# A third of the softmax pieces of eight blocks go to tiles of another pool, and expert numbers are read one by one

## The chip, the cores and the metric

The kernel runs on one core of a Trainium2 chip. Its engines each work through a list of their own, in order: TensorE (PE; PEld is its weight load), VectorE (DVE), ScalarE (ACT), GpSimd (POOL) and SyncE (SP), which only issues DMAs and reads numbers into registers. An instruction that has to wait holds up everything behind it on its engine. The metric is device time in microseconds. Before the change three runs took 2329.93, 2331.04 and 2335.01 us; the median is 2331.04 us.

## The reference, cut to what matters

One layer of an encoder for 2048 tokens of 1024 numbers: a mixer (differential attention with 4 heads, and gated linear attention), cross-attention to 256 memory tokens, and a mixture of 32 experts of which each token takes two. The two parts that the change touches are these:

```python
# differential attention, 16 query blocks of 128, chunk-causal
def probs(qb, kk):
    sc = jnp.einsum('bhqd,bhkd->bhqk', qb, kk).astype(jnp.float32) * scale
    return jax.nn.softmax(jnp.where(mask, sc, -jnp.inf), axis=-1)
p = probs(qb1, k1) - lam * probs(qb2, k2)
o = jnp.einsum('bhqk,bhkv->bhqv', p.astype(v.dtype), v)
...
# experts: tokens sorted by expert, each expert's rows through its own three matrices
hid = jax.nn.silu(xb @ w_gate[e]) * (xb @ w_up[e])
out = hid @ w_down[e]
```

## The kernel before, in words

**Recording and order.** The kernel doesn't issue its instructions as it is written. It records them with what each needs, and `flush` then puts them in one order for each engine: it plays the program through with a price for each instruction (`price`) and, at each step, takes what can start first, with a recorded number plus a table of shifts to break ties. Tiles belong to tags (pools); those of one tag are opened strictly in the order in which they were recorded, each when a buffer of the tag is free in that play. So a price or a tile's tag changes the order of instructions on every engine, though not what they compute.

**Attention (`stage_a2`).** Query blocks go from 15 down to 0; block i sees (i+1)*128 keys. For each of 4 heads there are two score maps (s = 0, 1). `scores` multiplies queries `qT` with keys `KC` into PSUM banks `sc` (4 buffers, up to 512 keys each), VectorE takes the extreme of each (`mx`, `m`), and ScalarE writes the exponentials into the pieces `e`, one tile for each 1024 keys: two for blocks 15 to 8, one for blocks 7 to 0. All pieces come from tag "E", 8 buffers of 4 KB per partition. `combine` forms the difference of the two maps: VectorE into the first map's piece, ScalarE casts to half precision in the second map's piece, GpSimd writes the remainder there, and a DMA transposes the result to `pT`. `values` multiplies `pT` with values `VC`. A buffer of tag "E" is free when the GpSimd subtraction (first map) or the DMA transpose (second map) has read it.

**Tag "W".** 28 buffers of 4 KB. In attention they hold keys (`KC`, 8), values (`VC`, 8), the query weights `wq` (4) and the output weights `wo` (8). As the blocks go down, the keys and values of the highest blocks are used no more and their buffers come free. Recorded next on this tag, in `begin_c` ahead of block 0, are the cross-attention's keys `kv` (2) and query weights `wcq` (8), 512 KB each from memory.

**Cross-attention and routing (`stage_c`)** go block by block; each block's routing appends its tokens to the experts' lists in memory (`lists<-row,dest`, an indirect DMA from GpSimd, each after the one before has landed).

**Experts (`stage_moe`).** Experts 0 and 1 and a list of leftovers are fixed. Then `rank` sorts the other 30 by their number of tokens, and writes their numbers into the tile `order`. For each, `chosen` has SP read one number of `order` into a register (`value_load`; in the rows TENSOR_LOAD, then a register operation and a check, ISA), `fetch` loads 128 list entries at a time (`lt<-lists`) and gathers the tokens (`ex<-xnS,lt`, tag "Q", 4 buffers), and `split_expert` loads the expert's weights in 12 pieces of 512 KB (`est`, tag "E", 8 buffers), which ScalarE and VectorE split into two half-precision parts (`ew`, tag "W"). The register tells where `lt` and `est` read. All `est` and `lt` are issued from SP. `fetch` is called two experts ahead of use.

Of the kernel before, what the change touches and what calls it, by code (L numbers as in the profile page):

```python
# [19 lines left out]
S = 2048  # L20
# [16 lines left out]
PT0 = 1  # L37
AHEAD = 4
GATE0 = 6
FTAG = "W"  # L40
# [64 lines left out]
class Program:  # L105
# [121 lines left out]
    def price(self, o, outs, ins):  # L227
# [3 lines left out]
        if m == "value_load":  # L231
            return 100
        if o.dma:
# [164 lines left out]
class Layer:  # L398
# [541 lines left out]
    def stage_a2(self):  # L940
# [4 lines left out]
        self.wo = [self.stored("wo", self.woS[4 * n:4 * n + 4]) for n in range(2)]  # L945
        blocks = self.blocks
        heads = [(j, h) for j in range(NB) for h in range(4)]
        for x, y in zip(heads + [None], [None] + heads):
# [72 lines left out]
    def scores(self, B, h, s):  # L1021
# [19 lines left out]
        self.prog.group = "se" if n > 1024 else "SE"  # L1041
        e = B["e", h, s] = [self.tile("E", "e", [w], F32) for _, w in B["chunks"]]
        for c, (b, k0, w) in enumerate(sc):
# [435 lines left out]
    def stage_moe(self):  # L1479
# [3 lines left out]
        slots += [k + j * n for k in range(n) for j in range(3)]  # L1483
        ready, rows = {}, {}

        def fetch(n):

            s = slots[n]
            if n == 0:
                which, need = lambda: NE, ()  # L1490
            elif n < FIXED:
                which, need, _ = self.second
            else:
                if n == FIXED:
                    self.rank()
                which, need = self.chosen(s)
            self.prog.shift = FRONT
            rows[n] = which, need, self.fetch(CAPS[s], which, need)
            self.prog.shift = 0

# [17 lines left out]

    def chosen(self, rank):

        reg = []
        need = [self.prog.call("sync", lambda nc: reg.append(nc.sync.value_load(
            self.order[0:1, rank:rank + 1], min_val=0, max_val=NE - 1)), [], [self.order], method="value_load")]
        return (lambda: reg[0]), need
# [31 lines left out]
    def fetch(self, cap, which, need, first=None, blocks=0):  # L1556
# [4 lines left out]
        for t0 in range(0, cap, 128):  # L1561
# [7 lines left out]
            def load(nc, lt=lt, m=m, t0=t0, parts=parts):  # L1569
# [7 lines left out]
                if parts > 1:  # L1577
# [3 lines left out]
            x = self.tile("Q", "ex", [2, D], F16)  # L1581
            prog.call("gpsimd", lambda nc, x=x, lt=lt, g=g: nc.gpsimd.indirect_dma_start(  # L1582
                out=x[:g].rearrange("p t d -> p (t d)"), out_offset=None, in_=self.xnS[:S + OFF - blocks * 128],
                in_offset=bass.IndirectOffsetOnAxis(ap=lt[:g, 0:1], axis=0)), [x[:g]],
                      [lt[:g], self.xnS[:S + OFF - blocks * 128]])
            rows.append((t0, n, x, m, lt, parts))
# [133 lines left out]
```

## Time and profile before

| | us |
|---|---|
| median of three runs | 2331.04 |
| profiled execution | 2337.98 |
| its span | 2336.2 |
| PE busy | 2133.3 (91%) |
| DVE busy | 1543.2 (66%) |
| ACT busy | 1341.4 (57%) |
| POOL busy | 775.1 (33%) |

The span is the profiled execution from its first instruction to its last, and 1.78 us of the execution lie around it. Busy shares are means over stages that have different limits: attention runs from about 620 to 1200 us, cross-attention from there to about 1600, the experts from there to the end. Block 11's scores begin at about 810 us, block 7's at 965, block 3's at 1070.

### The profile page before, as it was taken

To read this page: it belongs to the slowest core of one execution; us is meant where nothing else is said; L and a number is where in the kernel's file an instruction comes from. 1 tells how busy PE (TensorE), PEld (TensorE's weight loads), DVE (VectorE), ACT (ScalarE), POOL (GpSimd) and SP (SyncE) were. 2 spreads that over 40 slices of the span, in tenths; PEclk is the share of its full clock that TensorE was granted. 3 is DMA by queue.
4 is the path that set the end of the run, shared out by engine and by line. 5 is a ranking of instruction groups with operands and counts; after the bars stand their busy time and mean duration, and the time that the engine had idled before them with its cause. 6 is when DMAs were issued, how large, how long until landed. Compare 5 with 4: busy or idle time off the path is not lost.

```text
span 2336.2 us, 56192 instructions
## 1 busy us (share of the span) xinstructions
PE 2133.3 (91%) x22161; PEld 1463.9 (63%) x22161; DVE 1543.2 (66%) x3439; ACT 1341.4 (57%) x2850; POOL 775.1 (33%) x814
## 2 busy tenths in 40 slices
PE   6999998999988888889998999997699999999898
PEld 3456655565544544545575777865587877777776
DVE  7354355654578878887645665458477878877884
ACT  6455355554466666666433333345477777777774
POOL 1445235552155555455312222213221222222201
PEclk9999999999989999999999999998899999999999
DMA  9544346674457777677984675574799999999995
GB/s 259 158 119 105 95 114 190 187 204 119 119 110 152 154 162 163 155 174 181 207 209 121 141 168 115 125 215 141 248 327 352 361 353 366 359 349 359 361 357 143
DMA packets 500089, 484.52 MB, mean 207 GB/s; under 512 B 387202, under 2 KB 397596, under 8 KB 499820
## 3 DMA queue, kind: packets, MB, share of 16 engines
q1 hardware_dynamic: 485788, 441.06, 64.7%
q0 software_dynamic: 14032, 39.82, 7.1%
q8 instruction: 175, 2.87, 0.5%
q14 instruction: 94, 0.77, 0.1%
HBM read 306.35 MB, written 83.74 MB: 167 GB/s over the span
## 4 chain that ended last, share of the span: by engine, by line
PE 40%; DVE 8%; DMA 7%; issue 3%; ACT 3%; POOL 2%; SPq 1%; POOLq 0%; ACTq 0%; DVEq 0%
PE pgu L171 13%; PE py L171 8%; PE phc L171 6%; PE pc L171 6%; PE ph L171 2%; DMA est<-in_w_e_down_dram 2%; DVE mx L171 2%; ACT ew L171 2%; PE pxT L171 2%; PE pcs L171 2%; DMA pT<-e 1%; DVE e L171 1%; DMA xTr<-xc 1%; DVE ew L171 1%; PE sc L171 1%
## 5 line engine op out<-in xcount | busy, mean ns | idle before, releaser
L171 DVE SCALAR_TENSOR_TENSOR ew<-est,ew 128x1024 f16<-128x1024 f32 x384 | 461.5, 1220 | 97.8 <-ACT ew L171 88.0
L171 PE MATMUL pgu<-exT,ew 128*128 128x160 f16 (+27 forms) x6336 | 446.4, 225 | 3.0 <-issue 2.2
L171 PEld LDWEIGHTS <-ew 128*128 128x128 f16 x6336 | 403.9, 98 | 11.3 <-issue 4.8
L171 ACT ACTIVATE ew<-est 128x1024 f16<-128x1024 f32 x384 | 395.2, 1051 | 13.8 <-DMA est<-in_w_e_down_dram 7.8
L171 PEld LDWEIGHTS <-uT 128*128 128x128 f16 x1920 | 187.2, 98 | 226.0 <-issue 9.8
L171 POOL TENSOR_TENSOR e<-e 128x256 f16<-128x256 f32 (+1 forms) x288 | 201.0, 727 | 190.9 <-ACT e L171 107.7
L171 PE MATMUL py<-ew,hid 128*128 128x512 f16 (+4 forms) x1560 | 245.4, 349 | 19.7 <-DVE hid L171 14.3
L171 DVE TENSOR_REDUCE mx<-sc 128x1 f32<-128x512 f32 (+3 forms) x320 | 185.5, 603 | 67.9 <-PE sc L171 67.4
L171 ACT ACTIVATE e<-sc,m 128x512 f32<-128x512 f32 (+3 forms) x288 | 179.0, 630 | 73.2 <-DVE m L171 34.6
L171 PE MATMUL sc<-KC,qT 128*128 128x512 f16 (+3 forms) x640 | 174.9, 367 | 42.7 <-ACT e L171 40.3
L171 PE MATMUL ph<-wo,mT 128*128 128x512 f16 x768 | 193.9, 383 | 9.6 <-DMA mT<-gS 4.7
L171 PE MATMUL pc<-hT,wcq 128*128 128x128 f16 x3072 | 191.2, 219 | 1.4 <-DMA hT<-hcS 0.8
L171 PEld LDWEIGHTS <-wcq 128*128 128x128 f16 x3072 | 179.8, 98 | 4.7 <-DMA hT<-hcS 1.3
L171 PEld LDWEIGHTS <-hid 128*128 128x128 f16 (+4 forms) x1560 | 105.7, 104 | 120.7 <-issue 17.9
L171 PE MATMUL phc<-wco,prT 128*128 128x512 f16 x768 | 176.5, 383 | 4.3 <-DMA prT<-prc 4.3
L171 PE MATMUL po<-VC,pT 128*128 128x128 f16 x1632 | 130.2, 226 | 9.6 <-DMA pT<-e 5.0
L171 PEld LDWEIGHTS <-pT 128*128 128x128 f16 x1632 | 109.7, 102 | 37.5 <-DMA pT<-e 14.6
L171 PEld LDWEIGHTS <-prT 128*128 128x128 f16 x768 | 74.3, 99 | 86.5 <-DMA prT<-prc 4.4
L1660 POOL DMA_INDIRECT out_dram<-ey,lt x33 | 55.5, 1681 | 219.6 <-ACT ey L171 191.4
L1582 POOL DMA_INDIRECT ex<-xnS,lt x52 | 63.9, 1228 | 194.2 <-PE pxT L171 139.1
L171 PEld LDWEIGHTS <-mT 128*128 128x128 f16 x768 | 72.7, 98 | 86.2 <-DMA mT<-gS 7.0
L171 PEld LDWEIGHTS <-qT 128*128 128x128 f16 x640 | 60.4, 101 | 97.2 <-issue 57.7
(324 smaller groups left out, 3671.6 us busy)
## 6 DMA issues: line engine op xcount, KB each, us to landing
est<-in_w_e_gate_dram SPq DMA_DIRECT2D x128, 512.0 KB
est<-in_w_e_up_dram SPq DMA_DIRECT2D x128, 512.0 KB
est<-in_w_e_down_dram SPq DMA_DIRECT2D x128, 512.0 KB
wst<-in_w_in_dram SPq DMA_DIRECT2D x20, 512.0 KB
xt<-in_x_dram SPq DMA_DIRECT2D x16, 512.0 KB
uS<-uT SPq DMA_DIRECT2D x16, 512.0 KB
ust<-in_w_ckv_dram SPq DMA_DIRECT2D x16, 512.0 KB
uT<-uS SPq DMA_DIRECT2D x16, 512.0 KB
```

What stands on the lines that cost most here:

```text
L171: o.fn = fn or (lambda nc: getattr(getattr(nc, eng), method)(*a, **k))
L1582: prog.call("gpsimd", lambda nc, x=x, lt=lt, g=g: nc.gpsimd.indirect_dma_start(out=x[:g].rearrange("p t d -> p (t d)"), out_offset=None, i ...
L1660: self.prog.call("gpsimd", lambda nc: nc.gpsimd.indirect_dma_start(out=out, out_offset=bass.IndirectOffsetOnAxis(ap=rows, axis=0), in_=y, ...
```

## The change

Two edits. First, for blocks 11 to 4 every third piece `e` (counted over all blocks) is a tile of tag "W" in place of "E". Second, the read of a ranked expert's number is priced at 570 in place of 100 in the ordering, and from the third ranked expert on it needs, in the ordering, the token gather of the expert two places ahead of it; so the 30 reads don't stand side by side any more. No instruction is added or taken away.

```diff
+FEWER = range(4, 12)
...
         if m == "value_load":
-            return 100
+            return 570
...
+        self.made = 0
...
-        e = B["e", h, s] = [self.tile("E", "e", [w], F32) for _, w in B["chunks"]]
+        e = B["e", h, s] = []
+        for _, w in B["chunks"]:
+            self.made += 1
+            tag = "W" if self.made % 3 == 0 and B["i"] in FEWER else "E"
+            e.append(self.tile(tag, "e", [w], F32))
...
-        ready, rows = {}, {}
+        ready, rows, gathers = {}, {}, []
...
-                which, need = self.chosen(s)
+                which, need = self.chosen(s, gathers[n - 2:n - 1] if n > FIXED + 1 else [])
...
             rows[n] = which, need, self.fetch(CAPS[s], which, need)
+            gathers.append(self.gathered)
...
-    def chosen(self, rank):
+    def chosen(self, rank, after):
...
-            self.order[0:1, rank:rank + 1], min_val=0, max_val=NE - 1)), [], [self.order], method="value_load")]
+            self.order[0:1, rank:rank + 1], min_val=0, max_val=NE - 1)), [], [self.order], after, method="value_load")]
```

Line numbers of the changed kernel are higher by 1 to 9. Where the instructions went is seen at three places.

SP before, where the ranked experts begin: after the last weights of expert 1 that could be issued, 30 reads of `order` stand in a row (L1522), then ten loads of lists (L1579), and only then weights again (L1547).

```order
L1547 DMA est_3276<-in_w_e_down_dram 128x1024
L1522 TENSOR_LOAD order_3352
L1522 ISA x2
...
L1579 DMA lt_3337<-lists_1034 128x1x2
L1579 DMA lt_3339<-lists_1034 128x2
...
L1579 DMA lt_3481<-lists_1034 128x1x2
L1547 DMA est_3278<-in_w_e_down_dram 128x1024
L1547 ISA
L1547 DMA est_3387<-in_w_e_gate_dram 128x1024
```

The same place on SP now: two reads (L1531), seven loads of lists (L1588), then the same weights.

```order
L1556 DMA est_3276<-in_w_e_down_dram 128x1024
L1531 TENSOR_LOAD order_3352
L1531 ISA x2
...
L1588 DMA lt_3337<-lists_1034 128x1x2
L1588 DMA lt_3339<-lists_1034 128x2
...
L1588 DMA lt_3385<-lists_1034 128x1x2
L1556 DMA est_3278<-in_w_e_down_dram 128x1024
L1556 ISA
L1556 DMA est_3387<-in_w_e_gate_dram 128x1024
```

28 reads and three loads of lists have left the place between `est_3276` and `est_3278`.

SP now, further on, between an expert's weights: each of the 28 reads stands with its expert's one or two loads of lists, among the 12 weight pieces of another expert.

```order
L1556 DMA est_3438<-in_w_e_gate_dram 128x1024
L1531 TENSOR_LOAD order_3352
L1531 ISA x2
L1588 ISA
L1588 DMA lt_3432<-lists_1034 128x2
...
L1588 DMA lt_3481<-lists_1034 128x1x2
L1556 ISA
L1556 DMA est_3440<-in_w_e_gate_dram 128x1024
```

Before, these loads of lists stood among the weights too, without a read.

SP before, in attention while block 5 and block 4 are worked on: the last two of the ten cross-attention loads, `wcq`, stand alone between transposes; the eight others stand in the same way in earlier blocks.

```order
L171 DMA hcS7_1134<-hc_2087 128x2048
L171 DMA wcq_2503<-wcqS6_154 128x2048
L171 DMA_TRANSPOSE pT_2211<-e_2202 128x12x128
L171 DMA_TRANSPOSE mT_2165<-mcd_2164 128x8x128
L171 DMA wcq_2504<-wcqS7_155 128x2048
L171 DMA_TRANSPOSE pT_2234<-e_2216 128x12x128
L171 DMA_TRANSPOSE mT_2246<-gS5_102 128x8x128
L171 DMA_TRANSPOSE qT_2224<-qc_2223 128x16x128
```

The same place now (`qT_2224` is the transposed query of block 3):

```order
L172 DMA_TRANSPOSE mT_2246<-gS5_102 128x8x128
L172 DMA kv0_2495<-kvS0_268 128x2048
L172 DMA kv1_2496<-kvS1_269 128x2048
L172 DMA wcq_2497<-wcqS0_148 128x2048
...
L172 DMA wcq_2502<-wcqS5_153 128x2048
L172 DMA_TRANSPOSE qT_2224<-qc_2223 128x16x128
L172 DMA uT_2298<-uS2_83 128x2048
L172 DMA wcq_2503<-wcqS6_154 128x2048
```

All ten loads of tag "W" now come after the last piece `e` of that tag; eight of them stand side by side ahead of the query of block 3, and the two others soon after. In attention from block 11 to block 1 the order on PE, DVE, ACT and POOL differs too; in cross-attention, to the first gathers of the experts, it is the same on every engine.

## Rows read from the trace of the kernel before

**Rows 1.** Busy time by stage: stretch, us, each engine (x instructions), clock, DMA share, GB/s.
```profile
core 0: us, PE busy (x) PEld busy (x) DVE busy (x) ACT busy (x) POOL busy (x), PEclk, DMA share, GB/s
795.00:965.00 170.00, 144.26 (x1056) 82.29 (x1056) 135.89 (x293) 108.54 (x280) 86.50 (x115) 0.94 0.73 158
965.00:1085.00 120.00, 103.77 (x756) 57.75 (x754) 100.13 (x249) 78.78 (x205) 61.73 (x80) 0.97 0.75 168
1085.00:1200.00 115.00, 112.90 (x1092) 75.00 (x1090) 73.09 (x210) 55.70 (x149) 40.36 (x54) 1.00 0.85 185
1200.00:1560.00 360.00, 352.17 (x4096) 260.25 (x4094) 195.70 (x703) 135.57 (x350) 80.77 (x123) 0.99 0.62 152
1625.00:1655.00 30.00, 11.97 (x74) 5.33 (x75) 11.58 (x41) 4.57 (x9) 8.47 (x6) 0.69 0.13 30
1690.00:2280.00 590.00, 556.21 (x7312) 452.46 (x7311) 464.28 (x631) 447.52 (x669) 130.31 (x87) 0.97 1.02 355
```

**Rows 2.** SP in order of time, 1616 to 1658: start, us, instruction.
```profile
1616.96 5.29 SPq L1547 DMA_DIRECT2D est<-in_w_e_down_dram  x3
1646.13 6.50 SPq L1579 DMA_DIRECT2D lt<-lists  x10
1652.74 0.40 SPq L1547 DMA_DIRECT2D est<-in_w_e_down_dram  x1
1653.41 3.88 SPq L1547 DMA_DIRECT2D est<-in_w_e_gate_dram  x4
```

**Rows 3.** The reads of line 1522: count, duration ns, first and last start us.
```profile
L1522 SPq TENSOR_LOAD <-order x30: 261/266/476, 1628.3 to 1645.4; - x30
```

**Rows 4.** Other engines in order of time, 1609 to 1651, idle before in brackets.
```profile
1609.67 0.96 POOL L1403 DMA_INDIRECT lists<-row,dest  x1 [1.41 <-DMA lists<-row,dest]
1621.83 7.18 POOL L1403 DMA_INDIRECT lists<-row,dest  x1 [1.60 <-DMA lists<-row,dest]
1628.10 0.17 DVE L171 CAST order<-prk 1x32 int32<-1x32 f32 x1
1648.59 0.21 DVE L171 TENSOR_SCALAR dst<-lt,part 128x1 int32<-128x1 int32 x1 [14.88 <-DMA lt<-lists]
1650.67 6.05 PE L171 MATMUL py<-ew,hid 128*128 128x512 f16 x50 [14.34 <-DVE hid L171]
```

**Rows 5.** What SP waited for, 1690 to 2280: us in total, times, longest.
```profile
SPq L1547 <- DVE ew L171: 161.5, 155, 3.7
```

**Rows 6.** The chain of waits: start, us, what.
```profile
1743.83 7.54 DMA lt<-lists
```

**Rows 7.** Waits of ACT and PE, 795 to 965: us in total, times, longest.
```profile
ACT e L171 <- POOL e L171: 10.3, 8, 1.9
ACT e L171 <- DMA pT<-e: 8.1, 3, 4.8
PE sc L171 <- ACT e L171: 20.6, 16, 3.7
```

**Rows 8.** ACT and PE in order of time, two of those waits each.
```profile
825.21 0.69 ACT L171 ACTIVATE e<-sc,m 128x512 f32<-128x512 f32 x1 [1.76 <-POOL e L171]
826.04 0.59 PE L171 MATMUL sc<-KC,qT 128*128 128x512 f16 x2 [1.70 <-ACT e L171]
...
962.06 0.69 ACT L171 ACTIVATE e<-sc,m 128x512 f32<-128x512 f32 x1 [4.78 <-DMA pT<-e]
962.89 0.59 PE L171 MATMUL sc<-KC,qT 128*128 128x512 f16 x2 [1.21 <-ACT e L171]
```

**Rows 9.** Cross-attention's loads, then block 3's query and the first scores that use it.
```profile
L171 SPq DMA_DIRECT2D kv<-kvS x2: 324/324/325, 748.0 to 791.4; - x2
...
L171 SPq DMA_DIRECT2D wcq<-wcqS x8: 324/450/531, 813.8 to 1072.2; - x8
...
1084.98 1.88 SPq L171 DMA_TRANSPOSE qT<-qc  x1
...
1089.35 0.38 PE L171 MATMUL sc<-KC,qT 128*128 128x512 f16 x1
```

More of the change, by code (lines that the diff above doesn't have):

```diff
@@ L1581, in fetch @@
             x = self.tile("Q", "ex", [2, D], F16)
-            prog.call("gpsimd", lambda nc, x=x, lt=lt, g=g: nc.gpsimd.indirect_dma_start(
+            self.gathered = prog.call("gpsimd", lambda nc, x=x, lt=lt, g=g: nc.gpsimd.indirect_dma_start(
                 out=x[:g].rearrange("p t d -> p (t d)"), out_offset=None, in_=self.xnS[:S + OFF - blocks * 128],
                 in_offset=bass.IndirectOffsetOnAxis(ap=lt[:g, 0:1], axis=0)), [x[:g]],
-                      [lt[:g], self.xnS[:S + OFF - blocks * 128]])
+                                      [lt[:g], self.xnS[:S + OFF - blocks * 128]])
             rows.append((t0, n, x, m, lt, parts))
```

## The prediction

> **What bounds the kernel now.** I read the busy times by stage first, then, where a stage has a hole, each engine in order of time, and last the waits. In the table by stage [rows 1] the reader is to see four different limits. From 795 to 1085 us, in attention, no engine is full: PE is busy 144.26 of 170 us and DVE 135.89 of 170, then 103.77 and 100.13 of 120, so waits between engines set the pace. From 1085 to 1560 PE is busy 112.90 of 115 and 352.17 of 360 us: PE is the limit. From 1625 to 1655 nothing is: PE is busy 11.97 of 30 us and the DMA engines 0.13 of the time. From 1690 to 2280 the DMA engines show a share of 1.02 at 355 GB/s: transfers set the pace there, with PE close behind (556.21 of 590).
>
> The hole at 1625 to 1655 has one cause in SP's list. SP ends its last weight issue at 1616.96 + 5.29 = 1622.25 and issues its next DMA at 1646.13 [rows 2]. In between stand the 30 reads, from 1628.3 to 1645.4 [rows 3]: 17.1 us for 29 steps, 0.59 us each, of which the load itself is 0.266 and the rest is what goes with it. They could start when VectorE had written `order`, at 1628.10 [rows 4]. While they run, VectorE waits 14.88 us for a list that SP has not asked for, and TensorE 14.34 us for VectorE [rows 4]. So the last thing to end is SP's row of reads, and everything else is behind it.
>
> **Part one: the reads.** Now two reads stand there, and they end at 1628.3 + 2 x 0.59 = 1629.5. What is late next is the lists: the last scatter into them is on GpSimd from 1621.83 for 7.18 us, to 1629.01, and such a scatter landed 1.41 to 1.60 us after its issue ended [rows 4], so at about 1630.5. The first list load moves from 1646.13 to some 1630.6, 15.5 us earlier. Ten list loads took 6.50 us [rows 2], 0.65 each; seven now take 4.6, so the first weights go at 1635.2 where they went at 1652.74, 17.5 us earlier. Their buffers are free by then: VectorE's splits of what had been loaded were through but for one, which stood behind the wait of 14.88 us itself. I take the middle of the two shifts, 16.5 us, with 15.5 and 17.5 as ends.
>
> Does this reach the end? The list of work behind it is the same, and from 1655 on the DMA engines are full to 2280 [rows 1], so a stream of equal length that starts 16.5 us sooner ends 16.5 us sooner. If it is TensorE that paces some of that stage, it starts as much earlier, since its wait of 14.34 us ends with the same list.
>
> What comes back: the other 28 reads, 28 x 0.59 = 16.5 us on SP, now among the weight issues. The trace has no read of `order` inside that stage, so I bound it: nothing, if SP waits anyway, and 16.5 us, if each read delays the stream by its length. SP waits there for buffers that VectorE frees, 161.5 us in 155 waits [rows 5], so it is ahead of the stream; eight buffers of 512 KB in turn are 8 x 524288 bytes / 355 GB/s = 8 x 1.48 = 11.8 us of transfers, against a delay of 0.59 us once in an expert. That row is much nearer to nothing: I take 1 us. What is queued behind a read on SP are the list loads of the same expert and then weight pieces; who waits for them are the gather on GpSimd and the splits on ScalarE. The list is read an expert ahead of its gather, so I cost its later place at nothing here, and as a rival below. The one read of `total` (for the loop after the experts) moves up a little past weight pieces; it needs a sum that VectorE makes a few us after its wait ends, before SP gets there: nothing.
>
> Part one: 16.5 - 1 = 15.5 us, between -1 and 17.5.
>
> **Part two: the pieces of tag "W".** An exponential waits for a buffer when ScalarE waits for GpSimd's subtraction or for a transpose to read an older piece. Between 795 and 965 us these waits are 10.3 us in 8 and 8.1 us in 3 [rows 7], together 18.4. All lie in blocks 11 to 8, which take two pieces for each map; in blocks 7 to 4, one piece each, the same view shows none, so half of the edit has nothing to remove. What counts is whether PE then waits too. Of its 20.6 us behind ScalarE's exponentials [rows 7], six waits end 0.6 to 0.9 us after such a wait of ScalarE; the first and the last are the pairs in [rows 8], 1.70 and 1.21 us, and the six add up to 8.0. With a third of the pieces elsewhere, eight buffers serve twelve pieces, three heads in place of two, and I expect these waits to go. The gain is between nothing (VectorE, 80% busy, becomes what ScalarE waits for) and 18.4; I take 8, what PE itself waited.
>
> The same edit moves the ten loads of cross-attention's keys and weights. Before, they were issued one by one from 748.0 to 1072.2 [rows 9]; now eight stand ahead of block 3's query on SP. They are 8 x 1.48 = 11.8 us of transfers at the rate of the experts' stage, and in the trace that query had no slack: its transpose was issued at 1084.98 and the scores that use it ran at 1089.35 [rows 9]. The cost is between a gain (each earlier single load no longer stands before a transpose, up to 1.48 each, of which I count nothing) and 11.8 us, if the whole run is before the query and PE has nothing else. PE has output products and values to run in that place, and the loads can go while SP waits for the query; I take 4, a third, as nearer to the row that shows PE full there (112.90 of 115). Their own need is far off, in cross-attention.
>
> Part two: 8 - 4 = 4 us gained, between a loss of 12 and a gain of 18. It reaches the end because PE is the limit from 1085 to 1560 and its order there from block 0 on is unchanged.
>
> **Sum.** 15.5 + 4 = 19.5 us. The profiled execution took 2337.98 us (span 2336.2 and 1.78 around it), so 2318.5 in such an execution. The median of the three runs is 2331.04, 6.94 below the profiled one; I carry the same gain to it: 2311.5 us.
>
> **Rivals.**
> - *Attention loses.* The run of eight loads holds block 3's query, and the transposes behind it, for most of its 11.8 us, and the freed waits of ScalarE turn into waits for VectorE: a loss of 6 in place of a gain of 4. For it: no slack in [rows 9]. Against: PE's other work there. 2331.0 - 15.5 + 6 = 2321.5.
> - *Attention gains all of it.* All 18.4 us of buffer waits come off and the loads hide: 2331.0 - 15.5 - 18.4 = 2297. Against: VectorE at 80%, and five of the eleven waits had no wait of PE behind them.
> - *The reads are paid in full.* Each of the 28 holds the weight stream for its 0.59 us: 16.5 us come back, and attention's 4 are left, 2327. For it: the eight buffers may all be in use when SP reads. Against: [rows 5]. The Trainium skill (DMA: Bandwidth & Descriptors, section "Latency and other measured facts") gives a floor of about 600 ns for each such load, wherever it stands; the 0.59 us here agree, and by that rule alone an estimated 28 x 0.6 = 16.8 us stay on SP, and whether they are hidden no run here shows yet.
> - *The stall isn't the reads.* The lists land as late as before, and the reads only stood beside that wait. Then three list loads (2 us) and attention's 4 are won: 2325. Against: SP's first list load came 0.1 us after the last read's 0.59 us were over (1645.4 + 0.59 against 1646.13).
> - *Lists become the wait, and it is slower.* Read one by one, each list is loaded into full queues: one took 7.54 us to land and stood in the chain of waits [rows 6]. If its expert's gather waits for it, TensorE waits for the gather. From 19.5 / 28 = 0.7 us of open wait in each of 28 experts on, the change is slower; at 1 us it costs 28, and 2331.0 - 19.5 + 28 = 2339.5. Against: the order puts the read an expert ahead, some 20 us (590 us for 29 experts), against 7.54. The skill's same section has 2 us for a memory access at high load; the 7.54 us are far above it, and the measured one decides.
>
> **Chances.** Forecast 0.55, with a range of its own from 2303 to 2319 (attention from 12 gained to 4 lost). Attention loses 0.17, attention gains all 0.10, the reads paid in full 0.07, the stall isn't the reads 0.06, lists make it slower 0.05. The range 2300 to 2326 leaves out most of the case at 2297, the one at 2327 and the one at 2339.5, together under 0.2. A difference under 0.2%, 4.7 us, can't be told from none. Faster by more than that (under 2326.4): the forecast, both cases of attention, and about half of the two at 2325 and 2327, 0.88. Within it: the rest of those two, 0.07. Slower: 0.05.
>
> **What would show it.** Right on part one: SP's first ranked weights 17 us sooner after `order` is written than the 24.6 us of before (1628.10 to 1652.74), hence about 7; no wait of VectorE near 14.88 us; the stage at 355 GB/s as long as before. Wrong, if GB/s there falls with SP busy in reads, or GpSimd's gathers wait for lists far more than before. Right on part two: fewer waits of ScalarE for GpSimd and transposes between 795 and 965, and block 7's scores some 8 us sooner; then a wait of PE for block 3's query of about 4 us. The forecast is wrong as a whole if less than 10 us are gained between the write of `order` and the end, or attention loses more than 6.

## The result, and the profile after

| | before | after |
|---|---|---|
| median of four runs, us | 2330.83 | 2299.14 |
| lowest to highest, us | 2329.93 to 2335.01 | 2296.29 to 2301.12 |
| profiled execution, us (span) | 2337.98 (2336.2) | 2296.29 (2294.4) |

The ratio is 0.9866, with an interval of 95% from 0.9844 to 0.9888: 31.7 us faster, 1.3%. The prediction was 2311.5 us, a gain of 19.5; the direction is right, and the time lies under the predicted range.

The two profiled executions differ by 41.8 us of span. Cut at the first mask matmul of block 11, the last one of block 0, the write of `order`, the first ranked weight behind it and the last weight, that is:

| stretch | before, us | after, us | gained |
|---|---|---|---|
| start to block 11 | 817.69 | 819.85 | -2.2 |
| blocks 11 to 0 | 363.28 | 340.13 | 23.2 |
| end of block 0 to the write of `order` | 447.1 | 445.9 | 1.2 |
| write of `order` to first ranked weight | 24.64 | 6.77 | 17.9 |
| first ranked to last weight | 639.26 | 637.61 | 1.6 |
| last weight to the end | 44.2 | 44.1 | 0.1 |

So there are two gains, one of each edit. Before's profiled execution is 7 us above its median and after's is the lowest of its four, so about 10 of the 41.8 us are the scatter of executions.

**The reads.** The reads and the write of `order` in the changed kernel (count; shortest, median and longest duration in ns; first and last start in us), against [rows 3]:

```profile
L1531 SPq TENSOR_LOAD <-order x30: 270/460/1194, 1606.1 to 2175.2; - x30
L172 DVE CAST order<-prk x1: 172/172/172, 1605.9 to 1605.9; 1x32 int32<-1x32 f32 x1
```

The 30 reads no longer stand in a row of 17 us: they are spread over 570 us. SP in order of time there (start, us, instruction), against [rows 2]:

```profile
1594.77 5.29 SPq L1556 DMA_DIRECT2D est<-in_w_e_down_dram  x3
1608.01 4.58 SPq L1588 DMA_DIRECT2D lt<-lists  x7
1612.69 0.41 SPq L1556 DMA_DIRECT2D est<-in_w_e_down_dram  x1
1613.37 2.75 SPq L1556 DMA_DIRECT2D est<-in_w_e_gate_dram  x4
```

The first list goes 2.1 us after the write of `order` and the first weight 6.8 us after it. What is late now is the last scatter into the lists, as the prediction said; on GpSimd it is this row, against [rows 4]:

```profile
1598.75 8.07 POOL L1410 DMA_INDIRECT lists<-row,dest  x1 [0.72 <-DMA lists<-row,dest]
```

It ends at 1606.82, and SP's first list load follows at 1608.01, after a wait of 0.3 us for this scatter to land; so the two reads and the scatter now end almost together. VectorE's wait of 14.88 us for a list has become the wait of 1.9 us in this row (what VectorE waited for, 1600 to 1660 us: us in total, times, longest):

```profile
DVE dst L172 <- DMA lt<-lists: 1.9, 1, 1.9
```

And the stage behind it has the same rate as in [rows 1] (stretch, its length, busy time of each engine with its instructions, granted clock, share of the DMA engines, GB/s):

```profile
1603.00:1633.00 30.00, 20.74 (x354) 15.23 (x351) 18.77 (x57) 13.49 (x26) 11.14 (x8) 0.85 0.69 215
1648.00:2238.00 590.00, 562.71 (x7388) 457.61 (x7386) 468.74 (x640) 450.16 (x676) 133.29 (x88) 0.98 1.02 357
```

The 28 reads in it did not lower the 355 GB/s of before. SP still waits there for buffers, as in [rows 5] (us in total, times, longest, 1648 to 2238 us):

```profile
SPq L1556 <- DVE ew L172: 170.5, 166, 3.7
```

It is ahead of the stream, with reads or without.

**The pieces.** The same view by blocks: 11 to 8, 7 to 4, and the sum with blocks 3 to 0. First the kernel before:

```profile
817.69:979.62 161.93, 137.20 (x1014) 78.55 (x1013) 129.78 (x281) 103.03 (x261) 81.39 (x109) 0.94 0.72 160
979.62:1089.56 109.94, 96.80 (x710) 53.68 (x709) 89.67 (x225) 71.65 (x186) 58.04 (x76) 0.98 0.78 174
...
sum 363.28, PE 323.60 PEld 186.45 DVE 278.77 ACT 217.51 POOL 171.84; mean PE 107.87 PEld 62.15 DVE 92.92 ACT 72.50 POOL 57.28
```

Then the changed kernel:

```profile
819.85:951.59 131.74, 119.54 (x937) 68.24 (x936) 123.97 (x271) 100.46 (x258) 83.26 (x107) 1.00 0.85 173
951.59:1070.27 118.68, 108.04 (x810) 60.98 (x809) 95.09 (x245) 73.88 (x191) 58.46 (x79) 1.00 0.83 193
...
sum 340.13, PE 314.26 PEld 181.68 DVE 276.25 ACT 216.40 POOL 172.32; mean PE 104.75 PEld 60.56 DVE 92.08 ACT 72.13 POOL 57.44
```

Blocks 11 to 8 are 30.2 us shorter and blocks 7 to 4 are 8.7 longer. The counts of TensorE say that these 8.7 are no loss: 77 fewer matmuls stand in the first stretch and 100 more in the second. TensorE had filled its waits with other blocks' products, and these now come later. So it is the sum that counts, and it splits in two. TensorE's idle time went from 363.28 - 323.60 = 39.7 us to 340.13 - 314.26 = 25.9, which is 13.8 us. Its busy time for nearly the same work fell by 9.3 us; the granted clock of blocks 11 to 8 went from 0.94 to 1.00. As an estimate from the traces: over the three stretches TensorE was busy for 21.7 us at a clock of 0.50 before and for 3.4 us after, and half of the difference, 9.1 us, is what the slow clock cost, nearly all of the 9.3.

One pair of executions is little for that split. Of the runs below, the reads alone, the reads doubled and the second profile of before have, in attention, the order of instructions of the kernel before on all four engines; the pieces alone, the price alone, one read and three reads have that of the changed kernel. Blocks 11 to 0 take 358.8 to 363.3 us in the four profiles with the old order and 338.9 to 346.3 in the five with the new. By the means, 361.9 and 342.5, that is 19.4 us, of which 12.4 are TensorE's idle time and 7.0 its busy time (worked out as above, an estimated 6.2 of these are the clock's).

The waits of the changed kernel in blocks 11 to 8, against [rows 7]:

```profile
ACT e L172 <- DVE m L172: 19.9, 19, 2.6
ACT e L172 <- DVE e L172: 9.8, 13, 1.8
...
PE sc L172 <- ACT e L172: 7.1, 9, 2.2
```

ScalarE's waits for GpSimd and for transposes, 18.4 us of buffers, are gone altogether, and VectorE is what ScalarE waits for now. TensorE's waits behind exponentials, 20.5 us in blocks 11 to 8 before, are 7.1: not 8 of them went but 13.4. Of the 20.5 us only 8.1 stood right behind a buffer wait of ScalarE, the rest mostly behind its waits for VectorE; so at least 5.3 of the 13.4 us that went were not buffer waits themselves.

Where the clock's part comes from shows in stretches of 4 us. The kernel before, from 840 to 860:

```profile
840.00:844.00 4.00, 2.71 (x25) 1.59 (x24) 3.52 (x8) 2.85 (x8) 1.25 (x2) 1.00 0.78 148
844.00:848.00 4.00, 1.13 (x5) 0.33 (x5) 4.00 (x10) 2.00 (x4) 2.46 (x4) 0.95 0.74 180
848.00:852.00 4.00, 2.77 (x7) 0.89 (x7) 2.43 (x6) 2.33 (x8) 2.75 (x4) 0.50 0.63 118
852.00:856.00 4.00, 3.36 (x21) 2.26 (x21) 3.35 (x8) 2.93 (x8) 0.00 (x0) 0.50 0.08 17
856.00:860.00 4.00, 4.00 (x47) 3.21 (x45) 2.69 (x7) 1.78 (x5) 1.64 (x1) 0.77 0.55 105
```

After a hole in which TensorE was busy 1.13 of 4 us, the clock stands at 0.50, the level of 1.2 GHz, for some 10 us in all (by these rows), and these matmuls run slowly. The hole itself is not a buffer wait: TensorE's scores wait for an exponential, and the exponential stands on ScalarE behind a cast that waited for VectorE.

```profile
847.47 0.62 ACT L171 CAST e<-e 128x512 f16<-128x512 f32 x1 [2.00 <-DVE e L171]
848.85 1.44 PE L171 MATMUL sc<-KC,qT 128*128 128x512 f16 x3 [3.68 <-ACT e L171]
```

The changed kernel at its own emptiest place there:

```profile
844.00:848.00 4.00, 1.77 (x9) 0.69 (x8) 3.96 (x8) 3.58 (x8) 2.82 (x4) 1.00 0.21 39
848.00:852.00 4.00, 2.00 (x11) 0.73 (x11) 3.90 (x12) 2.39 (x8) 2.46 (x4) 1.00 0.69 131
```

The clock stays at 2.4 GHz here. The depth of the hole does not settle that: in the kernel with the pieces alone (below), which has the same order, TensorE was busy 1.77 and 2.20 us of 4 in a row there, and the next 4 us ran at 0.50. A fall behind this hole stands in all four profiles with the old order, and in three of the five with the new, there for some 7 us; with it blocks 11 to 8 took 133.8 to 134.4 us, without it 131.6 and 131.7. So the falls became fewer and shorter, and most of the 30 us in these blocks was gained even where this one remained. From 841 to 871 us a score matmul of 128x512 took 483 ns before (first fence: line, shapes, count; busy us, mean ns; idle before) and 378 ns after:

```profile
L171 PE MATMUL sc<-KC,qT 128*128 128x512 f16 x28 | 10.7, 483 | 6.0 <-ACT e L171 6.0
```

```profile
L172 PE MATMUL sc<-KC,qT 128*128 128x512 f16 x37 | 11.2, 378 | 4.9 <-ACT e L172 4.8
```

**The loads of cross-attention** against [rows 9], on SP:

```profile
1052.81 1.05 SPq L172 DMA_DIRECT2D kv<-kvS  x2
1053.90 3.24 SPq L172 DMA_DIRECT2D wcq<-wcqS  x6
1057.26 9.28 SPq L172 DMA_TRANSPOSE qT<-qc  x1
```

Eight stand ahead of block 3's query, as forecast, and TensorE waits for that query at block 3's first score:

```profile
1070.04 0.39 PE L172 MATMUL sc<-KC,qT 128*128 128x512 f16 x1 [2.44 <-DMA qT<-qc]
```

That wait of 2.4 us is part of the 25.9 us above. Over blocks 11 to 0 TensorE's waits for queries rose from 1.2 to 6.1 us; in spite of them its idle time in blocks 7 to 4 fell from 13.1 to 10.6 us.

### The profile page after: what moved, and what is told of

Its sections match the earlier page's. It is cut to its first block, busy times and chain, and to the rows that moved or that the text cites. A ratio compares the mean times of both kernels' runs of the same rounds, so it can differ in the third digit from the quotient of the medians.

```text
span 2294.4 us, 56150 instructions
## 1 busy us (share of the span) xinstructions
PE 2128.3 (93%) x22161; PEld 1462.8 (64%) x22161; DVE 1540.9 (67%) x3439; ACT 1339.1 (58%) x2850; POOL 775.7 (34%) x814
## 4 chain that ended last, share of the span: by engine, by line
PE 40%; DMA 5%; ACT 3%; DVE 3%; issue 1%; SPq 0%; POOL 0%; POOLq 0%; DVEq 0%; ACTq 0%
PE pgu L172 13%; PE py L172 8%; PE pc L172 7%; PE phc L172 6%; PE pcs L172 2%; ACT ew L172 2%; PE ph L172 1%; PE pxT L172 1%; DMA xTr<-xc 1%; DMA est<-in_w_e_down_dram 1%; DVE ew L172 1%; DMA est<-in_w_e_up_dram 1%; DMA est<-in_w_e_gate_dram 0%; PE plg L172 0%; DMA ex<-xnS,lt 0%
## 5 line engine op out<-in xcount | busy, mean ns | idle before, releaser
L172 PE MATMUL sc<-KC,qT 128*128 128x512 f16 (+3 forms) x640 | 168.9, 360 | 32.9 <-ACT e L172 25.5
L172 PE MATMUL po<-VC,pT 128*128 128x128 f16 x1632 | 126.9, 223 | 10.2 <-DMA pT<-e 6.7
L172 POOL TENSOR_TENSOR uhl<-ust,uhl 128x1024 f16<-128x1024 f32 x44 | 94.8, 2161 | 57.3 <-ACT uhl L172 57.1
```

The costliest lines, as they stand in the source:

```text
L172: o.fn = fn or (lambda nc: getattr(getattr(nc, eng), method)(*a, **k))
```

## The experiments

Theory: the reads and the pieces are two gains that add; the reads shorten one stall and are hidden elsewhere; the pieces take buffer waits out of blocks 11 to 8, and with them a fall of TensorE's clock. The rivals are with each run. Edits are shown against the changed kernel unless another is named; every ratio is against the kernel before on the same chip, whose medians were 2333.81, 2335.19, 2335.39 and 2337.81 us in the four sets.

| kernel | median, us | ratio and interval |
|---|---|---|
| reads alone | 2323.62 | 0.9959 (0.9944 to 0.9973) |
| pieces alone | 2314.69 | 0.9919 (0.9904 to 0.9934) |
| reads, loads held back | 2342.18 | 1.0042 (1.0026 to 1.0058) |
| reads, pieces in 11 to 8 | 2303.26 | 0.9863 (0.9846 to 0.9881) |
| reads, pieces in 7 to 4 | 2329.13 | 0.9974 (0.9961 to 0.9987) |
| each number read three times | 2308.65 | 0.9889 (0.9868 to 0.9911) |
| pieces in 11 to 8, loads spread | 2306.55 | 0.9869 (0.9849 to 0.9889) |
| one read for all ranked experts | 2302.49 | 0.9859 (0.9835 to 0.9883) |
| price of a read alone | 2312.14 | 0.9899 (0.9875 to 0.9923) |
| every sixth piece, 11 to 8 | 2308.14 | 0.9887 (0.9867 to 0.9908) |
| every second piece, 11 to 4 | 2325.97 | 0.9967 (0.9950 to 0.9985) |
| before, reads doubled | 2352.22 | 1.0060 (1.0045 to 1.0075) |
| before, more matmuls | 2338.09 | 0.9989 (0.9974 to 1.0005) |

**The halves.** The reads alone:

```diff
-FEWER = range(4, 12)
+FEWER = range(0)
```

> All pieces stay in tag E; only the reads are changed. Theory A (the reads were a plain stall of 17.5 us, and all of it reaches the end): 17 to 19 us faster than before, and from the write of the expert numbers to the first weights that follow about 7 us in place of 24.6. Rival B (the two edits help each other, the reads alone are worth what was forecast for them less the cost of the 28 reads): 12 us or less. The sum with the run of the other half should give the 31.7 us of both.

The pieces alone:

```diff
-            return 570
+            return 100
-                which, need = self.chosen(s, gathers[n - 2:n - 1] if n > FIXED + 1 else [])
+                which, need = self.chosen(s, [])
```

> Only the pieces are changed; the 30 reads stand in a row as before. Theory A (the forecast of 4 us for attention was too small; the profiled executions differ by 22 us there): 13 to 22 us faster than before, block 7 begins 25 to 30 us sooner, and ScalarE waits for no buffer in blocks 11 to 8. Rival B (most of the 22 us is chance of two executions): 4 to 8 us faster.

The reads alone gain 10.2 us (by the interval 6.3 to 13.1) and the pieces alone 19.1 (15.4 to 22.4); together 29.3, near the 31.7 of both. On top of the pieces the reads are worth 12.4 us by the ratios (some 6 to 19). So the halves add, and the sizes of both were wrong in the forecast: the pieces are worth five times the 4 us, the reads two thirds of the 15.5.

**Which blocks.** The first with the pieces in blocks 11 to 8, the second in 7 to 4:

```diff
-FEWER = range(4, 12)
+FEWER = range(8, 12)
```

> Both edits, but only blocks 11 to 8 use tag W for every third piece. Theory A (blocks 7 to 4 showed no buffer waits): the same as the changed kernel within 3 us, or up to 8 us faster, since the changed kernel gave back 8.7 us between block 7 and block 3, where its loads stand in a row. Rival B (the pieces of blocks 7 to 4 carry their share of the gain): 8 us or more slower than the changed kernel.

```diff
-FEWER = range(4, 12)
+FEWER = range(4, 8)
```

> Both edits, but the pieces go to the other pool in blocks 7 to 4 alone. Theory: in those blocks no exponential waited for a buffer, so nothing is won there; blocks 11 to 8 take as long as before (161.9 us from the first mask of block 11 to that of block 7), and the time is that of the reads alone, 2323.6 us, up to 5 more if the ten loads, held back to a burst ahead of block 3's query, cost what blocks 7 to 4 gave back in the changed kernel (8.7 us): 2321 to 2330. Rival: every piece that leaves the pool helps in proportion, and a third of the 19.1 us comes from here: about 2317, with block 3 earlier by 6.

With blocks 11 to 8 alone the kernel is as fast as the changed one; with 7 to 4 alone it is no faster than the reads alone, rather some 3 us slower. Its blocks 11 to 8 and 7 to 4:

```profile
824.38:988.46 164.08, 138.25 (x1015) 79.92 (x1014) 130.37 (x281) 103.50 (x261) 82.40 (x109) 0.93 0.69 145
988.46:1103.09 114.63, 101.19 (x733) 56.00 (x732) 90.40 (x234) 72.26 (x186) 56.12 (x78) 0.99 0.85 191
```

Blocks 11 to 8 take 164 us with the clock at 0.93, as before, and blocks 7 to 4 win nothing: the prediction's reading that half of this edit has nothing to remove is shown.

**How many pieces.** Every sixth in blocks 11 to 8, then every second in 11 to 4:

```diff
-FEWER = range(4, 12)
+FEWER = range(8, 12)
-            tag = "W" if self.made % 3 == 0 and B["i"] in FEWER else "E"
+            tag = "W" if self.made % 6 == 0 and B["i"] in FEWER else "E"
```

> Both edits, with every sixth piece (not every third) of blocks 11 to 8 in the other pool: ten or eleven of 64 in place of 21. Theory: the waits for buffers go piece by piece: half of the 20.5 us that blocks 11 to 0 gained with every third are left, 2313, and TensorE's clock in the slice from 841 to 871 us lies between 0.83 and 1.00. Rival: a few more buffers are enough, since the waits are short: the same as with every third, 2303. Rival two: a pair of pieces is only as early as its later one, and a sixth wins nothing: 2323.

```diff
-            tag = "W" if self.made % 3 == 0 and B["i"] in FEWER else "E"
+            tag = "W" if self.made % 2 == 0 and B["i"] in FEWER else "E"
```

> The changed kernel with every second piece of blocks 11 to 4 in the other pool. Theory: with every third no exponential of blocks 11 to 8 waits for a buffer any more, and VectorE is busy 29 of 30 us from 871 to 961, so there is nothing left to win: 2299 within 4. Rival: blocks 7 to 4 still want buffers: 2294. Rival two: more pieces in that pool hold the loads of cross-attention back further: 2304.

Half as many pieces keep most of the gain, between the theory and the first rival ("the same as with every third"). Blocks 11 to 8 then take 141.9 us, with the clock between the two others:

```profile
815.55:957.46 141.91, 127.05 (x957) 71.82 (x956) 125.83 (x279) 101.30 (x259) 85.03 (x109) 0.96 0.81 175
```

Every second piece came out 24 us slower than every third by the ratios; the second rival, the only one that had a loss, had 5. Block 3 starts as early as in the changed kernel (1069.20 against 1070.27), and then blocks 3 to 0 take 111 us in place of 90, at a clock of 0.94:

```profile
1069.20:1180.25 111.05, 97.69 (x766) 58.55 (x765) 60.81 (x168) 43.74 (x117) 31.53 (x40) 0.94 0.81 199
```

Not all of these 21 us are the loads': 48 more matmuls stand there than in the changed kernel (766 against 718), left over from blocks 11 to 4. But its loads stand at 1067 to 1092 on SP, 15 us later than in the changed kernel and among the transposes of blocks 3 and 2:

```profile
1067.46 0.91 SPq L172 DMA_DIRECT2D kv<-kvS  x2
1068.42 2.39 SPq L172 DMA_DIRECT2D wcq<-wcqS  x4
```

Length and buffer waits go together in these kernels, though not in step. ScalarE's buffer waits in blocks 11 to 8 are 18.4 us before (161.9 us), 4.7 with every sixth piece (141.9), 9.4 with every second (139.9) and none with every third (131.7). The planner changes the order of instructions along with the buffers, and no run holds one of them still. So it is shown that moving the pieces of blocks 11 to 8 brings the gain, and not shown how much of it the freed buffers bring and how much the other order.

**The loads.** The reads alone, with the ten loads held until block 4's last head (the same wait on the eight `wcq` loads):

```diff
-FEWER = range(4, 12)
+FEWER = range(0)
+            if (B["i"], h, s, c) == (4, 3, 0, 0):
+                self.mark = o
-            nc.sync.dma_start(KV[n], self.kvS[n])
+            self.prog.call("sync", lambda nc, n=n: nc.sync.dma_start(KV[n], self.kvS[n]), [KV[n]], [self.kvS[n]],
+                           [self.mark])
```

> Reads as in the changed kernel, all pieces in tag E, but the ten loads of cross-attention's keys and weights held back until block 4, head 3. To be held against the run of the reads alone. Theory A (buffers are what attention gained from): same as the reads alone within 4 us, the waits of ScalarE for buffers in blocks 11 to 8 stay near 18 us. Rival B (the transposes run better without the loads between them): 8 to 20 us faster than the reads alone.

That is 18.6 us slower than the reads alone. From block 11 to block 3 it keeps within 3 us of the reads alone, so the loads of before cost blocks 11 to 8 nothing and their going is no part of the gain. Blocks 3 to 0 take 112 us with the same number of matmuls as the reads alone, which need 91.8:

```profile
1087.35:1199.36 112.01, 94.72 (x741) 57.70 (x740) 60.32 (x168) 42.85 (x116) 32.40 (x40) 0.92 0.82 198
```

What TensorE waited for there:

```profile
PE sc L172 <- DMA qT<-qc: 8.6, 2, 7.9
PE pc L172 <- DMA hT<-hcS: 3.9, 1, 3.9
```

It is the kind of loss that the prediction's first rival named, loads ahead of a query, but the query of the 7.9 us is block 2's; block 3's was issued ahead of the loads. The first load is issued 1.6 us ahead of block 3's first mask matmul here, 1.7 us with every second piece, and 17.5 us in the changed kernel, where the loads come early enough. Spread over blocks 7 to 5, one behind each head:

```diff
-FEWER = range(4, 12)
+FEWER = range(8, 12)
+        self.turns = [(7, 1), (7, 2), (7, 3), (6, 0), (6, 1), (6, 2), (6, 3), (5, 0), (5, 1), (5, 2)]
+            if s == 0 and c == 0:
+                self.marks[B["i"], h] = o
-            nc.sync.dma_start(KV[n], self.kvS[n])
+            self.prog.call("sync", lambda nc, n=n: nc.sync.dma_start(KV[n], self.kvS[n]), [KV[n]], [self.kvS[n]],
+                           [self.marks[self.turns.pop(0)]])
```

> Both edits with the pieces in blocks 11 to 8 alone, and the ten loads of cross-attention's keys, values and weights issued one by one, each after the first exponential of one head from block 7's second to block 5's third. Theory: blocks 7 to 4 give back 6 to 9 us of what blocks 11 to 8 gain because the loads go there in a burst (share of the DMA engines 1.03 to 1.05 for 60 us) and hold the transposes; spread out they cost half of it: block 3 starts 3 to 5 us sooner than with the pieces in blocks 11 to 8 alone (1070.4), and the time is about 2299. Rival: the loads cost the same wherever they lie among these blocks, or blocks 7 to 4 give back for want of VectorE: 2303, block 3 at 1070.

The rival holds: 0.9869 is not told from 0.9863, and block 3 starts at 1076.2, not sooner. Among these blocks the place of the loads made no difference that the runs can tell.

**Are the reads hidden?** Each number read three times, then one number read once for all ranked experts, so that each of them loads the same expert's weights and the choice is left out:

```diff
+        for _ in range(2):
+            after = [self.prog.call("sync", lambda nc: nc.sync.value_load(
+                self.order[0:1, rank:rank + 1], min_val=0, max_val=NE - 1), [], [self.order], after,
+                method="value_load")]
```

> The changed kernel, but each of the 30 numbers is read three times (two more loads behind each, whose values nothing uses): 56 more reads among the weight issues, 4 more ahead of the lists. At 0.59 us each, the price that the row of 30 had, the 56 are 33 us of the sync engine. Theory: the sync engine is ahead of the weight stream, so reads there cost nothing; only the four ahead of the lists can show, up to 4 x 0.59 = 2.4 us: 2299 to 2303 us, and first to last weight of the experts' stage about 637.6 us, as in the changed kernel. Rival: each read holds the stream for its length, which would also explain why the reads alone won 10 us in the timed runs and not the 17.8 of the profiled ones: about 2299 + 33 = 2332 us, with first to last weight near 670. Half hidden: 2315.

```diff
+        if not hasattr(self, "reg"):
+            self.reg = reg = []
...
-        return (lambda: reg[0]), need
+        return (lambda: self.reg[0]), self.read + list(after)
```

> The changed kernel, but one number is read and serves all 28 ranked experts (28 times the same expert's weights; the choice is left out). The waits that hold each read until an earlier gather are kept, on the list load behind it. 28 reads fewer among the weight issues. Theory: they are hidden, so nothing changes: 2299 us within 3, first to last weight 637 to 640. Rival: they come back in part, which would be why the timed gain of the reads (10 us) is under the 17.8 us by which the first ranked weight moved: 6 us less, 2293. Paid in full: 28 x 0.59 = 16.5 less, 2282.5.

Three times as many reads cost 0.9889 - 0.9866 = 0.0023, 5 us and within the two intervals, of the 33 that the added ones among the weights last, and 2.0 of the 5 come from those ahead of the lists (first weight 8.81 us after `order`, not 6.77). With one read in place of 30 the ratio is 0.9859, not told from 0.9866. So the reads among the weights are hidden, all or most of them.

**What the waits on gathers do.** The planner's price alone:

```diff
-                which, need = self.chosen(s, gathers[n - 2:n - 1] if n > FIXED + 1 else [])
+                which, need = self.chosen(s, [])
```

> The changed kernel without the waits that hold each read until the gather of two experts before: only the planner's price of a read (570 in place of 100) is left, and the planner puts six reads ahead of the first lists and the other 24 within the first ten weight tiles. Theory: what counts is how many reads stand ahead of the first lists and weights: four more there, 4 x 0.59 = 2.4 us, less the 2.4 us for which the lists were waited for anyway, and the 24 among the first tiles, 14 us of reads while eight buffers of 1.48 us are empty and the stream has nothing queued: first ranked weight some 8 us after the order, and then a stream held for up to 14 us: between 2299 and 2314, I take 2306. Rival: the waits on gathers are what costs the reads' edit the rest of its 17.8 us: without them 2294.

It gives back about 8 us by the ratios, at the edge of what the intervals can tell and near the 7 of the middle that was expected, but in another place: the list loads became ten, with reads among them, and took 9.88 us, and the first weight went 15.25 us after `order` (1618.39), 8.5 later than in the changed kernel.

```profile
1622.49 9.88 SPq L1589 DMA_DIRECT2D lt<-lists  x10
1633.64 0.35 SPq L1557 DMA_DIRECT2D est<-in_w_e_down_dram  x1
```

**Why only 10 us of 17.9?** A second profile of the kernel before:

> The kernel before, unchanged, for a second profile: how much two profiled executions of one kernel differ, and where. The first profiled execution took 2338.0, 7 us over the median, that of the reads alone 2315.6, 8 us under its median. Theory: the 17.8 us between the write of the order and the first ranked weight are the same in every execution (24.6 us here again, within 0.3), and what scatters lies elsewhere. Rival: the row of reads itself is shorter in the median execution, some 17 us.

It took 2338.2 us; from `order` to the first weight it was 24.64 us again. What scatters is elsewhere: block 15 starts at 639.8 (634.7 in the first), and first to last weight is 635.3 us (639.3). So the 17.9 us are real. The kernel before with each number read twice:

```diff
             self.order[0:1, rank:rank + 1], min_val=0, max_val=NE - 1)), [], [self.order], method="value_load")]
+        need.append(self.prog.call("sync", lambda nc: nc.sync.value_load(
+            self.order[0:1, rank:rank + 1], min_val=0, max_val=NE - 1), [], [self.order], method="value_load"))
```

> The kernel before with each of the 30 numbers read twice in the row ahead of the lists: 30 more reads, 17.7 us at 0.59 each, so the first ranked weight goes some 42.3 us after the order in place of 24.65. Theory: the stretch between the order and the first ranked weight goes into the end one to one, in timed runs as in profiled ones, and the 10 us that the reads alone gained are a low draw: 17.7 us slower, ratio 1.0076. Rival: the stream behind takes part of it back (it starts with all of its buffers empty and their first experts split), so that only 0.6 of a shift arrives: 10 to 11 us slower, ratio 1.0045, with first to last weight 7 us shorter than the 635 to 639 of before.

The first weight goes 42.1 us after `order`, 17.5 later, and 14.0 us arrive at the end (10.5 to 17.5), between theory and rival. But the reads did not stay in one row. The planner put the first lists behind 31 of the 60, at 1645.86, where the first list of the kernel before went at 1646.13; the other 29 stand among the later lists and the first weights. So what came later are the weights and the later lists, not the first list, and this is not the old stall at double length. In the profile the stream behind is shorter, first to last weight:

```profile
1669.42:2301.40 631.98, 596.73 (x7911) 487.90 (x7911) 496.00 (x678) 477.14 (x719) 142.24 (x91) 0.97 1.02 354
```

Four profiles with a stall of 24.6 us have 635.3 to 639.3 us there, mean 637.1; nine with one of 6.8 have 635.9 to 643.8, mean 639.2. The 2.1 us between these means are within the scatter. The doubled reads lie 5.1 us under the first mean, but their stretch also holds 76 fewer matmuls than that of the kernel before (7911 against 7987) and 4.8 us less of TensorE's busy time, since that work ran ahead of the first weight. So a stream that takes back part of a stall is not shown. By the profiles 15.7 us of the reads' shift arrive; the timed runs show 10.2 for the reads alone and 12.4 on top of the pieces. The difference is open.

**Does the clock follow from the waits?** The kernel before with a fourth product in the values of blocks 11 to 8:

```diff
+                if 8 <= B["i"] < 12:
+                    nc.tensor.matmul(po[:, h], pT[:, nk + k], v[:, 1], start=False, stop=False)
```

> The kernel before with a fourth product in the values of blocks 11 to 8 (low part of the probabilities by low part of the values): 168 more matmuls of 128x128 there, 12.9 us of TensorE at the 77 ns that one took from the next (40.3 us of busy time in 525). The waits for buffers stay. Theory: TensorE's clock falls there because TensorE waits; with more work in the same waits it rises from 0.83 in the slice of 841 to 871, and the stretch from block 11 to block 7 grows by less than the work: 162 to 166 us, in all 2331 to 2338. Rival: the clock there has another cause and stays at 0.83: 162 + up to 12.9 = 170 to 175 us, in all 2341 to 2347.

168 more matmuls cost nothing that shows (0.9974 to 1.0005): the stretch of blocks 11 to 8 takes 160.4 us, and its busy time grew by 4.1 us for the 133 more matmuls in it, 10.2 us at the 77 ns expected for each:

```profile
824.75:985.11 160.36, 141.29 (x1147) 83.38 (x1146) 130.48 (x283) 104.44 (x261) 84.74 (x112) 0.96 0.77 160
```

By its time the theory holds; but the slice from 841 to 871 stays at 0.83, as the rival had it. Its rows of 4 us say why: the added work did not lie in that hole.

```profile
852.00:856.00 4.00, 0.32 (x2) 0.11 (x1) 3.54 (x8) 1.99 (x5) 3.51 (x5) 0.77 0.48 133
856.00:860.00 4.00, 2.99 (x9) 0.92 (x8) 2.87 (x7) 2.33 (x7) 1.71 (x3) 0.50 0.69 131
860.00:864.00 4.00, 4.00 (x25) 2.71 (x24) 2.80 (x6) 2.42 (x7) 0.00 (x0) 0.50 0.26 47
```

Again the fall to 1.2 GHz comes right behind the emptiest place. From 961 to 991 the clock, 0.94 in the kernel before, was 1.00, but there the order of the instructions differs too. So in these traces the falls come behind TensorE's holes; that filling a hole keeps the clock up is not shown.

None of these kernels is faster than the changed one by more than its interval.

## Why the prediction was wrong

- **Which two gains, and that they add:** right. The halves measured 10.2 and 19.1 us against 31.7 of both.
- **Where the reads' stall goes:** right. From `order` to the first weight 6.77 us against a forecast of about 7; the scatter into the lists is what is late next; the other reads are hidden, so the 1 us for them was near.
- **What arrives of it:** probably too much. The step was "a stream of equal length that starts 16.5 us sooner ends 16.5 us sooner". 15.5 us were forecast; the reads alone measured 10.2 (6.3 to 13.1), and on top of the pieces 12.4, whose interval holds 15.5. In the profiles the streams are of equal length within their scatter. Where the rest of the timed gain went is open.
- **The pieces:** this is the step that failed and that made the forecast too small: "I take 8, what PE itself waited", with 4 taken off for the loads. It was mis-sized; the place, blocks 11 to 8 and not 7 to 4, was right, and the buffer waits went. Measured are 19.1 us for the 4. The 8 counted only those waits of TensorE that ended within a microsecond of a buffer wait. In the profiles TensorE's idle time fell by 12.4 us, and in blocks 11 to 8 more of its waits went than had stood behind a buffer. Whether these went because the pieces came earlier or because the order is another, no run separates. And the forecast had no term for the clock at all, although [rows 1] show 0.94 in that stage: 7.0 us of busy time went with the new order, an estimated 6.2 of them the clock's.
- **The loads:** a wait for block 3's query came, 2.4 us at its first score for a forecast of 4. It did not show in the sum, since TensorE's idle time in those blocks fell all the same. The danger was real: issued 16 us later, counted from block 3's first mask matmul, the same loads cost 20 us.
- **The rivals:** nearest in time was "attention gains all of it", 2297. Its 18.4 us for the pieces are near the 19.1 measured, but by luck: they are what ScalarE waited for buffers, not what TensorE's idle time and clock gave. For the reads it had 15.5 us. VectorE, which spoke against it, did become what ScalarE waits for, but only behind the gain.
- **The rule on reads:** the Trainium skill (DMA: Bandwidth & Descriptors, section "Latency and other measured facts") gives a floor of about 600 ns for such a load. The trace agrees only for a whole read with its register operation and check, 0.59 us in the row; the load alone took 266 ns, and the measured one decides. By that rule an estimated 16.8 us (28 times 0.6) stay on SP; by the run with one read they are hidden there, all or most of them.

## What to carry to other kernels

When a buffer wait empties TensorE in a stage, price what the whole chain behind it loses, and look at the granted clock in stretches of a few microseconds right behind the hole: here TensorE's waits right behind buffer waits made 8 us and the attention blocks gave 19. When the start of a stream of weights moved, six to eight tenths of the shift arrived in the timed runs and nearly nine tenths in the profiles, so forecast a range and not the whole. When one pool's tiles go to another, look where that pool's next tenants are loaded: the same ten loads cost nothing that shows at one place, and 20 us when they came 16 us later.

## What was not expected of the hardware

- After 4 us in which TensorE was busy 1.13 us, its clock stood at 0.50 for some 10 us, and a 128x512 matmul took 483 ns on average in the 30 us around it, 378 where the clock held. Five profiles with one order of instructions had a fall at this place in three and none in two.
- A register load on SP took 266 ns in a row of its own and 460 ns (median; up to 1194) among weight issues, and was hidden there: 60 more of them, 35 us at the price of the row, moved the time by 5 us, within the two intervals.
- Two profiles of one kernel placed the same block 5 us apart, and its stream of weights took 635.3 and 639.3 us: differences of that size between two profiles say nothing of a change.
